# Attention logits in two 64-row tiles of TensorE, two query blocks at a time

## The chip, the cores and the metric

The program runs on one core of one Trainium2 chip. The metric is the device time of one execution in microseconds (us). Engines are named as in the profile: PE is TensorE's matmuls, PEld its weight loads, DVE is VectorE, ACT is ScalarE, POOL is GpSimd, and SP is the queue from which most transfers are issued.

## The reference

A two-layer trunk over a sequence of 2048 frames with width 1024. Layer 0 is a gated pooling mixer. Keys and values are then projected once, keys normalised per head, and layer 1 is a strictly causal stick-breaking attention with 16 heads of 64 elements. Cut to the part that the change touches:

```python
logits = einsum('bhtd,bhsd->bhts', q[:, :, t0:L], k[:, :, :L]) * SB_SCALE      # d = 64
mask = s_idx < t_idx
log_keep = where(mask, log_sigmoid(-logits), 0.0)
later = cumsum(log_keep, reverse=True) - log_keep
log_a = log_sigmoid(logits) + later
a = where(mask, exp(log_a), 0.0)
out = einsum('bhts,bhsd->bhtd', a, v[:, :, :L])
```

All is in 32-bit floating point. The logits contract over the 64 elements of a head only.

## The kernel before, in words

[...] To keep the precision, every operand is split into a high part and a low part (what the high part leaves over), and a product takes three passes: high x high, high x low, low x high.

The program has two parts. The first runs over four chunks of 512 frames (`s` = 0..3): it makes layer 0 and the projections, and writes the queries `qd`, keys `kd` and values `vd`, each as high and low parts, to device memory. The second is the attention. It runs over chunks of 512 queries (`c` = 3, 2, 1, 0), the 16 heads `h`, and chunks of 512 keys `kc` from `c` down to 0. Each triple is a *slot*; there are 64 + 48 + 32 + 16 = 160, and 64 of them (`kc == c`) are diagonal. A slot has four *units*, one for each block `j` of 128 queries. A loop over `n` counts the 640 units, and in each step it emits

- `turn` for the unit six steps back: transposes of 128x128 (L841) from SBUF into a PSUM tile `psa`, which ACT copies to the high part of `at` (L844) and DVE subtracts to the low part (L845);
- `front` for unit `n`: the logits into a PSUM tile `psl` (L816, L817), their sigmoid on ACT into `kap` (L820), and a running product along the keys on DVE into `pp` (L825 in a diagonal slot, L828 in another). In a diagonal slot block `j` has only `(j + 1) * 128` keys;
- a few pieces of the dense products that run beside the attention, from the generator `beside`: the gates `z` during chunk 3, and the output projection and gate of the chunk before during chunks 2, 1 and 0. One piece is one matmul of 128x512 (L885, L887, L889, tile `psd`); `rate` says how many go into a step;
- `gather` for the unit eight steps back: two matmuls with the values (L853, L854, tile `pso`).

When the last chunk's attention is through, the rest of its dense products follow alone.

The logits of a unit take two passes here, over all 128 rows of TensorE. `load_k` puts the key's high part on rows 0 to 63 and its low part on rows 64 to 127 of one tile `kk`. `load_q` makes `qa` (high above low) and `qb` (low above high). The first pass then sums high x high and low x low, and the second adds low x high and high x low. So two blocks take four passes.

There are two buffers of `psl`, two of `psa`, two of `pso`, and four of `kap`. The tiles of queries, keys and values come from one pool, `io`, of ten buffers of 2 KB a row; a slot's tiles are loaded one slot ahead by `begin`. The framework's scheduler sets the order on each engine from this program order, except where `stay` pins an instruction. Once per chunk `c`, `load_ends` makes four transposes of 8 rows (L802, tile `psae`).

Of the kernel before, what the change touches and what calls it, by code (L numbers as in the profile page):

```python
# [8 lines left out]
F32 = mybir.dt.float32  # L9
F32R = mybir.dt.float32r  # L10
# [4 lines left out]
P = 128  # L15
# [4 lines left out]
HD = 64  # L20
PLE = 256
W5 = 512
# [7 lines left out]
def f(ap):  # L30
    return ap.bitcast(F32)
# [3 lines left out]
def trunk_kernel(ctx, tc, x, p, a_norm, a_w_in, a_w_group, a_scale, a_w_out, kv_norm, w_kv,  # L35
                 k_norm, b_norm, b_w_in, b_q_norm, b_w_out, ple_w, ple_gate_w, out):
    nc = tc.nc
    V, A, G, T = nc.vector, nc.scalar, nc.gpsimd, nc.tensor
# [27 lines left out]
    qd = [[dram.tile([P, 2, W5], F32, name=f"qd{s}_{m}") for m in range(NH // 2)] for s in range(NSUB)]  # L66
# [72 lines left out]
    io = ctx.enter_context(tc.tile_pool(name="io", bufs=10))  # L139
# [5 lines left out]
        return act.tile([P, 2, W5], F32R, tag="act", name=nm)  # L145

    def load_q(c, h):
        qa = io.tile([P, W5], F32R, tag="io", name="qa")
        qb = io.tile([P, W5], F32R, tag="io", name="qb")
        rows = qd[c][h // 2][h % 2 * HD : (h % 2 + 1) * HD]  # L150
        for l in range(2):
            nc.sync.dma_start(out=f(qa)[l * HD : (l + 1) * HD], in_=rows[:, l])
            nc.sync.dma_start(out=f(qb)[(1 - l) * HD : (2 - l) * HD], in_=rows[:, l])
        return qa, qb

    def load_k(kc, h):
        kk = io.tile([P, W5], F32R, tag="io", name="kk")
        rows = kd[kc][h // 2][h % 2 * HD : (h % 2 + 1) * HD]
        for l in range(2):
            nc.sync.dma_start(out=f(kk)[l * HD : (l + 1) * HD], in_=rows[:, l])  # L160
        return kk

    def load_v(kc, h):
        vv = io.tile([P, 4, P], F32R, tag="io", name="vv")
# [14 lines left out]
    with ExitStack() as st:  # L179
# [548 lines left out]
        for i, (_, run) in enumerate(steps):  # L728
            after = steps[i + 1][0]() if i + 1 < len(steps) else None
            if after is None:  # L730
                early["q"] = load_q(NSUB - 1, 0)
                early["k"] = [load_k(NSUB - 1, 0), load_k(NSUB - 2, 0)]
                early["w"] = stored(wzd[0])
            run(*ready)
            if not i:
                load_gains([a_scale[0], b_norm[0], kv_norm], gains)
                load_head_gains()
            ready = after
            step, s = i % STEPS, i // STEPS
            if step >= 8 and (s + 1 < NSUB or step < 16):  # L740
                kept.pop(0)()
                if s + 1 < NSUB and step in (8, 12):
                    kept.pop(0)()
# [4 lines left out]
    with ExitStack() as st:  # L748
# [5 lines left out]
        psl = st.enter_context(tc.tile_pool(name="psl", bufs=2, space=bass.MemoryType.PSUM))  # L754
# [38 lines left out]
        def load_ends(c):  # L793
# [12 lines left out]

            return turned

        def front(st, j):

            w = (j + 1) * P if st["diag"] else W5
            r0 = W5 - w
            ps = psl.tile([P, W5], F32, tag="psl", name="psl")
            qs = slice(j * P, (j + 1) * P)
            (qa, qb), kk = st["q"], st["k"]
            T.matmul(ps[:, :w], qa[:, qs], kk[:, :w], start=True, stop=False)  # L816
            T.matmul(ps[:, :w], qb[:, qs], kk[:, :w], start=False, stop=True)  # L817
            kp = kaps[kcount[0] % NK]
            kcount[0] += 1
            A.activation(out=kp[:, r0:], in_=ps[:, :w], func=AF.Sigmoid, scale=-1.0)  # L820

            def scan():
                pp = ppool.tile([P, W5], F32, tag="pp", name="pp")
                if st["diag"]:
                    V.tensor_tensor_scan(out=pp[:, r0:][:, ::-1], data0=kp[:, r0:][:, ::-1],  # L825
                                         data1=ahead[:, r0:][:, ::-1], initial=1.0, op0=ALU.mult, op1=ALU.max)
                else:
                    V.tensor_tensor_scan(out=pp[:, ::-1], data0=kp[:, ::-1], data1=zeros.to_broadcast([P, W5]),  # L828
                                         initial=st["carry"][j], op0=ALU.mult, op1=ALU.add)
                st["carry"][j] = pp[:, r0 : r0 + 1]  # L830
                st["a"].append((pp, r0))

            return scan
# [190 lines left out]
        def begin(i):  # L1024
            c, h, kc = slots[i]
            if kc == c:
                if h == 1:
                    early["ends"] = load_ends(c)
                os = head["os"] if h % 2 else t2.tile([P, W5], F32, tag="os", name="os", bufs=9)
                head.clear()  # L1030
                head.update(q=early.pop("q", None) or load_q(c, h), carry=[None] * 4, o=[], os=os)
            kk = early["k"].pop(0) if early["k"] else load_k(kc, h)
            active[i] = dict(head, c=c, h=h, k=kk, v=load_v(kc, h), diag=kc == c, last=kc == 0, a=[], at={})

        for n in range(4 * len(slots) + LAG_G):
# [4 lines left out]
            i, j = divmod(n, 4)  # L1040
            scan = None
            if i < len(slots):
                c, h, kc = slots[i]
                if j == 0:
                    if i == 0:
                        begin(0)
                    if i + 1 < len(slots):
                        begin(i + 1)
                scan = front(active[i], j)
                if "ends" in early and j == 2:  # L1050
                    early.pop("ends")()
# [58 lines left out]
```

## Time and profile before

| what | value |
|---|---|
| time, median of 3 runs | 2767.84 us (2766.37 to 2770.78) |
| span of the profiled execution | 2765.4 us; that execution's own time is not given apart, and the median lies 2.4 us above its span |
| PE busy | 2725.7 us, 99% of the span, 13715 matmuls |
| PEld busy | 2260.4 us, 82% |
| DVE busy | 1956.0 us, 71% |
| ACT busy | 1385.5 us, 50% |
| POOL busy | 873.7 us, 32% |
| moved by DMA | 573.21 MB, 207 GB/s on average |
| granted TensorE clock | 0.999 |
| attention by chunk of queries, first to last `kap` | c = 3: 1365 to 1866 us; c = 2: to 2215; c = 1: to 2470; c = 0: to 2639 |

A row of the profile names the line, the engine, the operation, the tiles written and read, the shape, the count, the busy time in us and the mean duration of one in ns, and then the idle time before it with what ended it. Matmuls overlap: one of 128x512 lasts about 0.39 us in the records while the next starts 0.23 us after it, so the cost of a matmul is read from the distance between starts, not from its duration. A timeline row gives the start in us from the span's start, then the length, then the instruction; "x4" means four merged into one row.

### The profile page before, as it was taken

What the parts mean: (1) busy time and instruction counts of PE and PEld (TensorE: products, weight loads), DVE (VectorE), ACT (ScalarE), POOL (GpSimd) and SP (SyncE); (2) the same over time, 40 slices, a digit from 0 to 9 for tenths busy, and PEclk for the clock granted to TensorE, in tenths of its full rate; (3) what the DMA queues carried; (4) which work ended last, traced back from release to release, by engine and by line L of the source; (5) the groups of instructions that cost most, each with busy time, mean ns of one, the idle gap of its engine ahead of it and who ended that gap; (6) DMA issues with size and microseconds to landing.
All of it is one profiled execution on the core that took longest, in us unless ns stands there. A gap on an engine that the chain in (4) does not pass through costs nothing. (4 is left out here: it accounts for less than half of the span.)

```text
span 2765.4 us, 39537 instructions
## 1 busy us (share of the span) xinstructions
PE 2725.7 (99%) x13715; PEld 2260.4 (82%) x13715; DVE 1956.0 (71%) x2573; ACT 1385.5 (50%) x2801; POOL 873.7 (32%) x695
## 2 busy tenths in 40 slices
PE   9999999999999999999999999999999999999999
PEld 7888888888888888888888888887887778888877
DVE  6766535655357544565499999999999988996632
ACT  5444532445234542345356566666666655664521
POOL 2574338642475325753121111111110011112220
PEclk9999999999999999999999999999999999999999
DMA  8664696747946479445678565555555566668765
GB/s 293 236 196 171 218 325 204 225 148 253 347 148 227 163 249 318 136 145 170 191 254 278 180 217 170 169 161 178 169 159 162 159 200 200 188 204 264 249 209 160
DMA packets 335835, 573.21 MB, mean 207 GB/s; under 512 B 32462, under 2 KB 166638, under 8 KB 335636
## 3 DMA queue, kind: packets, MB, share of 16 engines
q1 hardware_dynamic: 330186, 563.03, 63.5%
q10 hardware_dynamic: 5450, 7.66, 0.9%
q8 instruction: 108, 1.77, 0.3%
q14 instruction: 91, 0.75, 0.1%
HBM read 430.01 MB, written 132.19 MB: 203 GB/s over the span
## 5 line engine op out<-in xcount | busy, mean ns | idle before, releaser
L844 ACT CAST at<-psa 128x512 fp32r<-128x512 f32 (+3 forms) x640 | 334.1, 522 | 478.4 <-PE psa L841 459.6
L536 PE MATMUL psd<-wpair,x 128*128 128x512 f32 x2304 | 544.0, 393 | 0.0
L828 DVE TENSOR_TENSOR_SCAN pp<-kap,pp,zeros 128x512 f32<-128x512 f32 x384 | 512.9, 1336 | 3.1 <-ACT kap L820 2.4
L536 PEld LDWEIGHTS psd<-wpair,x 128*128 128x128 f32 x2304 | 428.2, 188 | 86.2
L845 DVE TENSOR_TENSOR at<-psa,at 128x512 fp32r<-128x512 f32 (+3 forms) x640 | 381.0, 596 | 88.0 <-ACT at L844 84.9
L841 PE MATMUL psa<-ident,pp 128*128 128x128 f32 x2176 | 347.0, 275 | 17.2 <-DVE at L845 15.5
L820 ACT ACTIVATE kap<-psl 128x512 f32<-128x512 f32 (+3 forms) x640 | 344.9, 539 | 15.1 <-PE psl L817 12.0
L841 PEld LDWEIGHTS psa<-ident,pp 128*128 128x128 f32 x2176 | 262.9, 140 | 93.0 <-DVE at L845 38.8
L816 PE MATMUL psl<-kk,qa 128*128 128x512 f32 (+3 forms) x640 | 281.4, 440 | 0.0
L854 PE MATMUL pso<-at,vv 128*128 128x512 f32 (+3 forms) x640 | 235.1, 367 | 0.0
L817 PE MATMUL psl<-kk,qb 128*128 128x512 f32 (+3 forms) x640 | 233.0, 364 | 0.0
L853 PE MATMUL pso<-at,vv 128*128 128x512 f32 (+3 forms) x640 | 232.7, 364 | 0.0
L825 DVE TENSOR_TENSOR_SCAN pp<-kap,ahead 128x128 f32<-128x128 f32 (+3 forms) x256 | 219.8, 859 | 5.8 <-ACT kap L820 4.1
L131 PE MATMUL psd<-xp,wpair 128*128 128x512 f32 x512 | 201.9, 395 | 1.3 <-ACT xp L269 0.8
L132 PE MATMUL psd<-xp,wpair 128*128 128x512 f32 x512 | 200.5, 392 | 0.0
L133 PE MATMUL psd<-xp,wpair 128*128 128x512 f32 x512 | 200.1, 391 | 0.0
L113 DVE SCALAR_TENSOR_TENSOR wpair<-wraw,gains,wpair 128x512 fp32r<-128x512 f32 x192 | 169.7, 905 | 36.8 <-ACT wpair L112 36.1
L923 POOL TENSOR_TENSOR zr<-zr,sgz 128x512 f32<-128x512 f32 x32 | 58.8, 1836 | 368.2 <-ACT sgz L922 311.3
L112 ACT ACTIVATE wpair<-wraw,gains 128x512 fp32r<-128x512 f32 x192 | 135.0, 720 | 59.0 <-PE psd L536 32.3
L108 POOL TENSOR_TENSOR wpair<-wraw,wpair 128x512 fp32r<-128x512 f32 x99 | 145.5, 1485 | 59.7 <-ACT wpair L106 59.7
L853 PEld LDWEIGHTS pso<-at,vv 128*128 128x128 f32 x640 | 120.2, 188 | 26.9 <-ACT at L844 0.2
L854 PEld LDWEIGHTS pso<-at,vv 128*128 128x128 f32 x640 | 120.3, 188 | 25.9
(211 smaller groups left out, 5402.4 us busy)
## 6 DMA issues: line engine op xcount, KB each, us to landing
kk<-kd SPq DMA_DIRECT2D x320, 128.0 KB
vv<-vd SPq DMA_DIRECT2D x160, 256.0 KB
wraw<-in_w_kv_dram SPq DMA_DIRECT2D x128, 256.0 KB
wpair<-wzd SPq DMA_DIRECT2D x64, 512.0 KB
wpair<-wod SPq DMA_DIRECT2D x64, 512.0 KB
wpair<-wgd SPq DMA_DIRECT2D x64, 512.0 KB
wpair<-wu SPq DMA_DIRECT2D x48, 512.0 KB
wpair<-wi SPq DMA_DIRECT2D x36, 512.0 KB
```

The lines of the kernel that those rows point to most:

```text
L131: T.matmul(ps, wst(units, kt, 0, c0), acts[kt][:, 0], start=(begin and kt == order[0]), stop=False)
L536: T.matmul(pss2[i], ck["x2"][kt][:, xh, tk], wst(ws, kt, wh, 0, W5), start=(kt == 0 and xh == 0 and wh == 0), stop=(kt == KT - 1 and wh == 1))
L816: T.matmul(ps[:, :w], qa[:, qs], kk[:, :w], start=True, stop=False)
L817: T.matmul(ps[:, :w], qb[:, qs], kk[:, :w], start=False, stop=True)
L820: A.activation(out=kp[:, r0:], in_=ps[:, :w], func=AF.Sigmoid, scale=-1.0)
L825: V.tensor_tensor_scan(out=pp[:, r0:][:, ::-1], data0=kp[:, r0:][:, ::-1], data1=ahead[:, r0:][:, ::-1], initial=1.0, op0=ALU.mult, op1=AL ...
L828: V.tensor_tensor_scan(out=pp[:, ::-1], data0=kp[:, ::-1], data1=zeros.to_broadcast([P, W5]), initial=st["carry"][j], op0=ALU.mult, op1=AL ...
L841: T.transpose(pt[:, j * P : (j + 1) * P], pp[:, r0 + kt * P : r0 + (kt + 1) * P], ident)
L844: A.copy(out=at[:, 0, cs], in_=pt[:, cs])
L845: V.tensor_tensor(out=at[:, 1, cs], in0=pt[:, cs], in1=f(at[:, 0, cs]), op=ALU.subtract)
L853: T.matmul(po[:, cs], vv[:, kt, :], at[:, 0, cs], start=(st["diag"] and kt == 0), stop=False)
L854: T.matmul(po[:, cs], vv[:, kt, :], at[:, 1, cs], start=False, stop=(st["last"] and kt == 3))
```

## The change

Two blocks of queries, `j` and `j + 1` for even `j`, get their logits together, by two tiles of 64 rows of TensorE. The tile `e` = 0 stands on rows 0 to 63 and has block `j`; the tile `e` = 1 stands on rows 64 to 127 and has block `j + 1`. Each contracts over 64 rows, so it has three passes (high x high, low x high, high x low; low x low is left out), and the two tiles' passes alternate: six matmuls of 64 rows for two blocks, where four of 128 rows stood.

- `load_q` loads one tile `qt` with even blocks on the upper rows and odd blocks on the lower, high and low parts beside each other: four transfers of 64 KB for a head, in pieces of 512 bytes, where four of 128 KB stood.
- `load_k` loads two tiles, the high and the low part, each twice (on rows 0 to 63 and on rows 64 to 127): four transfers of 128 KB for a slot, where two stood. A slot takes two buffers of `io` for the keys where it took one, and a head one for the queries where it took two.
- `logits` takes both buffers of `psl` at once and writes them for two units; `front` calls it for even `j` only and uses one of the two tiles each time.

```diff
     def load_q(c, h):
-        qa = io.tile([P, W5], F32R, tag="io", name="qa")
-        qb = io.tile([P, W5], F32R, tag="io", name="qb")
-        rows = qd[c][h // 2][h % 2 * HD : (h % 2 + 1) * HD]
+        qt = io.tile([P, 2, 2, P], F32R, tag="io", name="qt")
+        rows = qd[c][h // 2][h % 2 * HD : (h % 2 + 1) * HD].rearrange("d l (g e q) -> e d l g q", e=2, q=P)
+        for e in range(2):
+            for l in range(2):
+                nc.sync.dma_start(out=f(qt)[e * HD : (e + 1) * HD, l], in_=rows[e, :, l])
+        return qt
...
+    def load_k(kc, h):
+        rows = kd[kc][h // 2][h % 2 * HD : (h % 2 + 1) * HD]
+        both = []
         for l in range(2):
-            nc.sync.dma_start(out=f(qa)[l * HD : (l + 1) * HD], in_=rows[:, l])
-            nc.sync.dma_start(out=f(qb)[(1 - l) * HD : (2 - l) * HD], in_=rows[:, l])
-        return qa, qb
...
-            nc.sync.dma_start(out=f(kk)[l * HD : (l + 1) * HD], in_=rows[:, l])
-        return kk
+            kk = io.tile([P, W5], F32R, tag="io", name="kk")
+            for e in range(2):
+                nc.sync.dma_start(out=f(kk)[e * HD : (e + 1) * HD], in_=rows[:, l])
+            both.append(kk)
+        return both
...
+        def logits(st, j):
+            pss = [psl.tile([P, W5], F32, tag="psl", name="psl") for _ in range(2)]
+            qt, (kh, kl) = st["q"], st["k"]
+            for i, (l, kk) in enumerate(((0, kh), (1, kh), (0, kl))):
+                for e in range(2):
+                    w = (j + e + 1) * P if st["diag"] else W5
+                    es = slice(e * HD, (e + 1) * HD)
+                    T.matmul(pss[e][:, :w], qt[es, l, j // 2], kk[es, :w], start=(i == 0), stop=(i == 2))
+            st["l"] = pss
+
         def front(st, j):
...
-            ps = psl.tile([P, W5], F32, tag="psl", name="psl")
-            qs = slice(j * P, (j + 1) * P)
-            (qa, qb), kk = st["q"], st["k"]
-            T.matmul(ps[:, :w], qa[:, qs], kk[:, :w], start=True, stop=False)
-            T.matmul(ps[:, :w], qb[:, qs], kk[:, :w], start=False, stop=True)
+            if j % 2 == 0:
+                logits(st, j)
+            ps = st["l"][j % 2]
```

The order of PE in the middle of chunk 3, before. `psa` are the transposes of an earlier unit, `psl` the logits, `psd` the pieces of the dense product, `pso` the products with the values:

```order
L841 MATMUL psa<-ident,pp 128x128 x4
L816 MATMUL psl<-kk,qa 128x512
L817 MATMUL psl<-kk,qb 128x512
L887 MATMUL psd<-xz,wpair 128x512
L889 MATMUL psd<-xz,wpair 128x512
L885 MATMUL psd<-xz,wpair 128x512
L853 MATMUL pso<-at,vv 128x512
L854 MATMUL pso<-at,vv 128x512
L841 MATMUL psa<-ident,pp 128x128 x4
L816 MATMUL psl<-kk,qa 128x512
L817 MATMUL psl<-kk,qb 128x512
```

The same place after (L855 was L841, L822 is the new line of the logits, L899, L901 and L903 were L885, L887 and L889, L867 and L868 were L853 and L854):

```order
L855 MATMUL psa<-ident,pp 128x128 x4
L822 MATMUL psl<-kk,qt 128x512 x6
L901 MATMUL psd<-xz,wpair 128x512
L903 MATMUL psd<-xz,wpair 128x512
L899 MATMUL psd<-xz,wpair 128x512
L867 MATMUL pso<-at,vv 128x512
L868 MATMUL pso<-at,vv 128x512
L855 MATMUL psa<-ident,pp 128x128 x4
L901 MATMUL psd<-xz,wpair 128x512
L903 MATMUL psd<-xz,wpair 128x512
L899 MATMUL psd<-xz,wpair 128x512
L867 MATMUL pso<-at,vv 128x512
```

The logits of two units stand together in every second unit, between a unit's transposes and a piece of the dense product; in the units between, the pieces follow the transposes directly.

ACT at such a place, before (`at` is the copy of transposes, `kap` the sigmoid of a unit's logits):

```order
L844 CAST at<-psa 128x512
L820 ACTIVATE kap_12820<-psl 128x512
L844 CAST at<-psa 128x512
L820 ACTIVATE kap_12821<-psl 128x512
L844 CAST at<-psa 128x512
L820 ACTIVATE kap_12822<-psl 128x512
```

And after (L858 was L844, L834 was L820):

```order
L858 CAST at<-psa 128x512 x2
L834 ACTIVATE kap_12825<-psl 128x512
L834 ACTIVATE kap_12826<-psl 128x512
L858 CAST at<-psa 128x512 x2
L834 ACTIVATE kap_12827<-psl 128x512
L834 ACTIVATE kap_12828<-psl 128x512
```

Copies and sigmoids alternate two by two where they alternated one by one; DVE's subtractions and running products do the same.

More of the change, by code (lines that the diff above doesn't have):

```diff
@@ L147, in load_q @@
     def load_q(c, h):
-        qa = io.tile([P, W5], F32R, tag="io", name="qa")
-        qb = io.tile([P, W5], F32R, tag="io", name="qb")
-        rows = qd[c][h // 2][h % 2 * HD : (h % 2 + 1) * HD]
-        for l in range(2):
-            nc.sync.dma_start(out=f(qa)[l * HD : (l + 1) * HD], in_=rows[:, l])
-            nc.sync.dma_start(out=f(qb)[(1 - l) * HD : (2 - l) * HD], in_=rows[:, l])
-        return qa, qb
[L156 to L159, printed above, removed]
-            nc.sync.dma_start(out=f(kk)[l * HD : (l + 1) * HD], in_=rows[:, l])
-        return kk
+        qt = io.tile([P, 2, 2, P], F32R, tag="io", name="qt")
[7 more added lines that the diff above has]
+        both = []
+        for l in range(2):
+            kk = io.tile([P, W5], F32R, tag="io", name="kk")
[3 more added lines that the diff above has]
+        return both
     def load_v(kc, h):
```

## The prediction

> **What bounds the kernel now.** I read the page's busy times first, then the costliest groups, then the busy time of each engine in the four stages of the attention, then PE's timeline where the logits stand.
>
> ```profile
> span 2765.4 us, 39537 instructions
> PE 2725.7 (99%) x13715; PEld 2260.4 (82%) x13715; DVE 1956.0 (71%) x2573; ACT 1385.5 (50%) x2801; POOL 873.7 (32%) x695
> L828 DVE TENSOR_TENSOR_SCAN pp<-kap,pp,zeros 128x512 f32<-128x512 f32 x384 | 512.9, 1336 | 3.1 <-ACT kap L820 2.4
> L816 PE MATMUL psl<-kk,qa 128*128 128x512 f32 (+3 forms) x640 | 281.4, 440 | 0.0
> L825 DVE TENSOR_TENSOR_SCAN pp<-kap,ahead 128x128 f32<-128x128 f32 (+3 forms) x256 | 219.8, 859 | 5.8 <-ACT kap L820 4.1
> ```
>
> PE is busy 99% of the span. The counts give the work: 640 units, of which 384 are full (L828) and 256 belong to 64 diagonal slots (L825). The stages of the attention, one for each chunk of queries from c = 3 to c = 0:
>
> ```profile
> core 0: us, PE busy (x) PEld busy (x) DVE busy (x) ACT busy (x) POOL busy (x), PEclk, DMA share, GB/s
> 1365.00:1866.00 501.00, 497.42 (x2707) 414.06 (x2706) 472.94 (x563) 300.11 (x598) 76.46 (x44) 1.00 0.65 204
> 1866.00:2215.00 349.00, 338.79 (x1880) 276.88 (x1879) 343.59 (x432) 226.33 (x466) 39.29 (x24) 1.00 0.55 166
> 2215.00:2470.00 255.00, 249.06 (x1388) 208.96 (x1386) 230.86 (x304) 154.34 (x335) 35.30 (x24) 1.00 0.65 196
> 2470.00:2639.00 169.00, 167.05 (x907) 141.32 (x905) 114.79 (x178) 85.11 (x205) 32.49 (x23) 1.00 0.79 245
> ```
>
> PE sets the pace in stages 3, 1 and 0. In stage 2 it is DVE (343.6 of 349 us), and PE idles 10.2 us there. So a change of PE's work counts in full in three stages; in stage 2 a gain is worth at most DVE's 5.4 us of idle time, and the first 10 us of a loss are hidden.
>
> **What the logits cost before.** A full unit of stage 3 on PE:
>
> ```profile
> 1701.24 0.60 PE L841 MATMUL psa<-ident,pp 128*128 128x128 f32 x4
> 1701.59 0.48 PE L816 MATMUL psl<-kk,qa 128*128 128x512 f32 x1
> 1701.91 0.39 PE L817 MATMUL psl<-kk,qb 128*128 128x512 f32 x1
> 1702.13 0.40 PE L887 MATMUL psd<-xz,wpair 128*128 128x512 f32 x1
> 1702.37 0.40 PE L889 MATMUL psd<-xz,wpair 128*128 128x512 f32 x1
> 1702.61 0.39 PE L885 MATMUL psd<-xz,wpair 128*128 128x512 f32 x1
> 1702.83 0.40 PE L853 MATMUL pso<-at,vv 128*128 128x512 f32 x1
> 1703.07 0.40 PE L854 MATMUL pso<-at,vv 128*128 128x512 f32 x1
> ```
>
> From L817 to L854 five starts take 1.16 us, so a pass of 128x512 costs 0.232 us whatever its duration. Two blocks of a full slot take four passes: 0.93 us. From the transposes to the second dense piece (L889) it is 1.13 us here; less the two passes of logits (0.464), 0.666 us is left for the transposes and one piece. Taken off the same stretch in a diagonal slot, that gives the narrower passes:
>
> ```profile
> 1707.44 0.60 PE L841 MATMUL psa<-ident,pp 128*128 128x128 f32 x4
> 1707.79 0.30 PE L816 MATMUL psl<-kk,qa 128*128 128x128 f32 x1
> ...
> 1708.33 0.39 PE L889 MATMUL psd<-xz,wpair 128*128 128x512 f32 x1
> ...
> 1709.26 0.60 PE L841 MATMUL psa<-ident,pp 128*128 128x128 f32 x4
> 1709.61 0.36 PE L816 MATMUL psl<-kk,qa 128*128 128x256 f32 x1
> ...
> 1710.17 0.39 PE L889 MATMUL psd<-xz,wpair 128*128 128x512 f32 x1
> ...
> 1711.09 0.60 PE L841 MATMUL psa<-ident,pp 128*128 128x128 f32 x4
> 1711.44 0.42 PE L816 MATMUL psl<-kk,qa 128*128 128x384 f32 x1
> ...
> 1712.11 0.39 PE L889 MATMUL psd<-xz,wpair 128*128 128x512 f32 x1
> ```
>
> 128 keys: 0.89 - 0.666 = 0.22 us for two passes; 256 keys: 0.24; 384 keys: 0.35. The first is hardly cheaper than the second: below 256 keys the weight load sets the pace, some 0.11 us each. The first two blocks of a diagonal slot take 0.47 us, the last two 0.35 + 0.46 = 0.82.
>
> **What a change of the tile's rows costs.** The kernel has one kind of matmul today that does not use all 128 rows: the four transposes of 8 rows (L802), and one of 24 rows early on (L657).
>
> ```profile
> 2226.69 0.40 PE L817 MATMUL psl<-kk,qb 128*128 128x512 f32 x1
> 2227.02 0.32 PEld L802 LDWEIGHTS psae<-ident,ends 8*128 8x128 f32 x4 [0.36 <-issue]
> ...
> 2227.36 0.19 PEld L885 LDWEIGHTS psd<-x,wpair 128*128 128x128 f32 x1
> 2227.36 0.50 PE L885 MATMUL psd<-x,wpair 128*128 128x512 f32 x1
> ...
> 2227.70 0.39 PE L887 MATMUL psd<-x,wpair 128*128 128x512 f32 x1
> ...
> 2473.70 0.34 PE L817 MATMUL psl<-kk,qb 128*128 128x384 f32 x1
> ...
> 2473.97 0.32 PEld L802 LDWEIGHTS psae<-ident,ends 8*128 8x128 f32 x4 [0.25 <-issue]
> ...
> 30.81 0.60 PE L206 MATMUL pst<-ident,rx 128*128 128x128 f32 x4
> ...
> 31.34 0.13 PEld L657 LDWEIGHTS pst<-ident,grow 24*128 24x128 f32 x1 [0.17 <-issue]
> ```
>
> Among matmuls of 128 rows the next weights load while the last matmul streams. Here they don't. After L817 (512 columns, 0.232 us) the 8-row weights start 0.33 us after its start, so 0.10 after its stream is over; after the one of 384 columns (0.175 us) they start at 0.27, again 0.10 after. After transposes of 128 rows the 24-row weights start 0.20 us after the start of the fourth (30.81 + 3 x 0.11 = 31.14), of which 0.11 is its own cost: 0.09. No engine or transfer is named as the releaser (the rows say "issue"). On the way out, L885's weights and its matmul both start at 2227.36, and the next starts 0.34 us later where 0.232 is usual: its weight load, hidden otherwise, shows with 0.105 us. So a change costs about 0.10 us of waiting, and the first weights after it stand exposed. The four 8-row loads take 0.32 us, 0.13 for the last, so they follow each other at 0.06 us.
>
> No row shows a tile of 64 rows. That a change between 128 and 64 rows waits as one between 128 and 32 or fewer does is taken from these rows as the nearest. [...]
>
> **The change part by part.** Every group of six matmuls stands between transposes and a dense piece, both of 128 rows, so it has two changes: 320 groups, 640 changes. For a weight load of 64 rows I take 0.06 (the 8-row loads) to 0.11 us (128 rows). The streams of the two tiles: 3 x 0.232 if they run side by side, 6 x 0.232 if one after the other. I take the first, since a pass costs by its columns and the tiles share neither rows nor output bank; the other end is a rival.
>
> - Full pairs, 192 groups: 0.10 (in) + one to two loads (0.06 to 0.22; the second tile may start one load later) + 0.70 + 0.10 (out) + 0.105 (exposed weights) = 1.06 to 1.22 us, against 0.93. That is +0.13 to +0.29, middle 0.21: +25 to +56 us, **+40**.
> - First two blocks of a diagonal slot, 64 groups: three passes of 256 columns (0.37) with one load, or six loads in a row (0.66) with a last pass of 0.12, beside 0.305 for the changes: 0.73 to 1.08, against 0.47. +0.26 to +0.61: +17 to +39 us, **+28**.
> - Last two blocks, 64 groups: 1.06 to 1.22 against 0.82: +0.24 to +0.40: +15 to +26 us, **+20**.
> - Cover in stage 2: **-10 us**, PE's idle time there.
> - Buffers of `psl`: a group needs both, so it waits for the sigmoid of the unit just before. In ACT's order the two sigmoids follow the group directly: some 0.2 + 2 x 0.60 us (0.61 in the stage's rows), while PE has at least two units of transposes, pieces and gathers, 2 x 1.6 us, until the next group. The cover is 1.8 us; if ACT's other work ate it, each group would pay up to its 0.6 us. I take nothing, and up to +10 us.
> - Keys are loaded in four transfers of 128 KB for a slot instead of two, queries in half the bytes. That is 160 x 256 KB - 64 x 256 KB = 25 MB more over 1274 us, 20 GB/s on 166 to 245. PE waits for no transfer there today and slots are loaded one ahead (about 8 us in stages 3 to 1). SP issues 320 more transfers, and behind them stand weights of the dense pieces. Nothing, with up to +5 us.
>
> Together 40 + 28 + 20 - 10 = **+78 us**, with bounds of +47 and +126. The profiled span of 2765.4 becomes 2843.4; the median lies 2.4 us over that span, so the time is **2846 us**.
>
> **The rivals.**
>
> *The change of rows costs nothing with 64-row tiles, and it is faster.* Then a full pair has three passes for four: -0.232 x 192 = -45 us; a diagonal slot -0.22 to +0.07, in the middle -5 us in all; of that, 10 us fall into stage 2, where DVE allows only 5 of 15. About -40 us: 2728. It decides at the point where the two changes of a group cost under 50 / 320 = 0.16 us together; the rows above give 0.31 and the first weights besides. For it speaks only that no row has 64 rows. Chance 0.10.
>
> *The two tiles don't run side by side*, and the changes cost as above. Six passes one after the other add 0.70 x 192 = 134 us in full pairs and some 0.8 x 64 = 51 in diagonal slots to the +78: about 3030 us. The trace has no two tiles in flight and is silent. [...] Chance 0.10.
>
> *One after the other, but no wait at the change*: (6 - 4) x 0.232 x 192 = 89 us, diagonal slots 0.63 x 64 = 40, less 10: +119, 2887. Chance 0.05. *Only the weights stand exposed and nothing drains*: 0.20 x 320 = 64 us less than forecast, about +16: 2784. Chance 0.05.
>
> **How the numbers follow.** The forecast has a chance of 0.70, with its own bounds from 2815 to 2894. Leaving out the first two rivals (0.10 each), the range takes in the other two: 2784 to 2894. A measurement of this kernel tells about 0.2% (5 us) from no change. Faster has the first rival and a little of small changes, 0.11; the same 0.02; slower 0.87.
>
> **What would show it.** Right: weights of the first 64-row matmul start about 0.2 us after the last transpose's start, and those of the dense piece after a group 0.33 us after the last logits matmul; the two tiles' matmuls start within 0.11 us of each other and the passes of one tile 0.23 us apart; stage 3 takes about 533 us, stage 2 365, stage 1 274, stage 0 181; DVE's idle time grows. Wrong: weights for 64 rows that load under the transposes before them; a group of six that takes 1.4 us of streams; PE waiting for ACT at the logits; or a stage 2 that grows as much as its PE work.

## The result and the profile after

The changed kernel takes 2836.1 us (median of 4 runs, 2835.71 to 2837.03) against 2768.0 us before in the same comparison: 1.0245 times as long, 95% interval 1.0230 to 1.0259, or +68 us. The forecast was 2846 us, +78.

The page's head and the group of the logits, and the four stages of the attention at their new bounds:

```profile
span 2834.4 us, 41303 instructions
PE 2796.6 (99%) x14355; PEld 2209.6 (78%) x14355; DVE 1965.2 (69%) x2573; ACT 1401.6 (49%) x2801; POOL 874.8 (31%) x695
L822 PE MATMUL psl<-kk,qt 64*128 64x512 f32 (+3 forms) x1920 | 295.7, 396 | 0.3
```
```profile
core 0: us, PE busy (x) PEld busy (x) DVE busy (x) ACT busy (x) POOL busy (x), PEclk, DMA share, GB/s
1366.00:1890.00 524.00, 521.82 (x2960) 389.85 (x2960) 477.59 (x564) 304.51 (x598) 76.27 (x44) 1.00 0.74 219
1890.00:2260.00 370.00, 360.78 (x2072) 262.42 (x2070) 344.64 (x430) 228.88 (x465) 38.11 (x23) 1.00 0.59 178
2260.00:2531.00 271.00, 265.40 (x1524) 200.13 (x1524) 236.68 (x308) 159.59 (x337) 36.38 (x24) 1.00 0.67 200
2531.00:2705.00 174.00, 171.74 (x946) 135.38 (x945) 112.40 (x174) 86.75 (x203) 32.56 (x23) 1.00 0.77 238
```

PE is still busy 99%, and PEld, with 640 loads more, is busy less. All four stages grew: 501 to 524, 349 to 370, 255 to 271, 169 to 174 us; outside the attention some 3 us were added. DVE's work is nearly the same and its idle time grew, from 28 to 46 us in stage 3 and from 5 to 25 in stage 2.

PE and PEld around one group, first of a full slot, then (PE only) of the first and of the last two blocks of a diagonal slot:

```profile
1705.68 0.60 PE L855 MATMUL psa<-ident,pp 128*128 128x128 f32 x4
...
1706.21 0.53 PEld L822 LDWEIGHTS psl<-kk,qt 64*128 64x128 f32 x6 [0.17 <-issue]
1706.21 0.96 PE L822 MATMUL psl<-kk,qt 64*128 64x512 f32 x6
...
1707.10 0.19 PEld L903 LDWEIGHTS psd<-xz,wpair 128*128 128x128 f32 x1 [0.36 <-issue]
1707.10 0.50 PE L903 MATMUL psd<-xz,wpair 128*128 128x512 f32 x1
...
1707.44 0.39 PE L899 MATMUL psd<-xz,wpair 128*128 128x512 f32 x1
```
```profile
1432.41 0.60 PE L855 MATMUL psa<-ident,pp 128*128 128x128 f32 x4
...
1432.94 0.62 PE L822 MATMUL psl<-kk,qt 64*128 64x128 f32 x6
...
1433.83 0.39 PE L901 MATMUL psd<-x,wpair 128*128 128x512 f32 x1
```
```profile
1436.12 0.60 PE L855 MATMUL psa<-ident,pp 128*128 128x128 f32 x4
1436.64 0.96 PE L822 MATMUL psl<-kk,qt 64*128 64x384 f32 x6
...
1437.88 0.40 PE L899 MATMUL psd<-x,wpair 128*128 128x512 f32 x1
```

The fourth transpose starts at 1706.01 (1705.68 + 3 x 0.11) and costs 0.11, so the weights at 1706.21 start 0.09 us after it: PE waits, with no releaser named. The first weights of both tiles load together, in the time of one:

```profile
1706.21 0.18 PEld L822 LDWEIGHTS psl<-kk,qt 64*128 64x128 f32 x2 [0.17 <-issue]
```

Six matmuls last 0.96 us together, where six in a row would have started over 1.16 us and then lasted 0.39 more: the tiles run side by side. The exit shows as forecast: the dense piece's weights and matmul start together at 1707.10, and the next one 0.34 us later. From the transposes to the second piece is 1.76, 1.42 and 1.76 us; less the 0.666 for transposes and a piece, a group costs **1.09, 0.75 and 1.09 us**, where the passes before cost 0.93, 0.47 and 0.82. Times 192, 64 and 64 groups that is 31 + 18 + 17 = 66 us more work for PE. The medians over all groups come to 1.09, 0.75 and 1.10 us, which makes 67.

### The profile page after: what moved, and what is told of

Same layout as the page of the kernel before. It is cut to its first block, busy times and chain, and to the rows that moved or that the text cites. A ratio compares the mean times of both kernels' runs of the same rounds, so it can differ in the third digit from the quotient of the medians.

```text
span 2834.4 us, 41303 instructions
## 1 busy us (share of the span) xinstructions
PE 2796.6 (99%) x14355; PEld 2209.6 (78%) x14355; DVE 1965.2 (69%) x2573; ACT 1401.6 (49%) x2801; POOL 874.8 (31%) x695
## 5 line engine op out<-in xcount | busy, mean ns | idle before, releaser
L858 ACT CAST at<-psa 128x512 fp32r<-128x512 f32 (+3 forms) x640 | 333.9, 522 | 456.6 <-PE psa L855 445.9
L842 DVE TENSOR_TENSOR_SCAN pp<-kap,pp,zeros 128x512 f32<-128x512 f32 x384 | 501.4, 1334 | 21.1 <-ACT kap L834 20.3
L859 DVE TENSOR_TENSOR at<-psa,at 128x512 fp32r<-128x512 f32 (+3 forms) x640 | 373.2, 596 | 108.9 <-ACT at L858 106.0
L834 ACT ACTIVATE kap<-psl 128x512 f32<-128x512 f32 (+3 forms) x640 | 320.3, 533 | 83.8 <-PE psl L822 71.7
L855 PE MATMUL psa<-ident,pp 128*128 128x128 f32 x2176 | 345.8, 274 | 13.3 <-DVE at L859 12.6
L855 PEld LDWEIGHTS psa<-ident,pp 128*128 128x128 f32 x2176 | 265.3, 141 | 81.7 <-DVE at L859 26.2
L822 PE MATMUL psl<-kk,qt 64*128 64x512 f32 (+3 forms) x1920 | 295.7, 396 | 0.3
L868 PE MATMUL pso<-at,vv 128*128 128x512 f32 (+3 forms) x640 | 234.4, 366 | 0.0
L867 PE MATMUL pso<-at,vv 128*128 128x512 f32 (+3 forms) x640 | 233.4, 365 | 0.0
L822 PEld LDWEIGHTS psl<-kk,qt 64*128 64x128 f32 x1920 | 158.9, 185 | 67.5 <-issue 52.0
L867 PEld LDWEIGHTS pso<-at,vv 128*128 128x128 f32 x640 | 120.4, 188 | 28.2 <-issue 1.5
L868 PEld LDWEIGHTS pso<-at,vv 128*128 128x128 f32 x640 | 120.5, 188 | 27.0
```

Of the source, the lines that this page charges most:

```text
L822: T.matmul(pss[e][:, :w], qt[es, l, j // 2], kk[es, :w], start=(i == 0), stop=(i == 2))
L855: T.transpose(pt[:, j * P : (j + 1) * P], pp[:, r0 + kt * P : r0 + (kt + 1) * P], ident)
L858: A.copy(out=at[:, 0, cs], in_=pt[:, cs])
L859: V.tensor_tensor(out=at[:, 1, cs], in0=pt[:, cs], in1=f(at[:, 0, cs]), op=ALU.subtract)
L867: T.matmul(po[:, cs], vv[:, kt, :], at[:, 0, cs], start=(st["diag"] and kt == 0), stop=False)
L868: T.matmul(po[:, cs], vv[:, kt, :], at[:, 1, cs], start=False, stop=(st["last"] and kt == 3))
```

## The experiments

The theory: the change of the tile's rows costs about 0.2 us each way, 640 times, and that is more than the passes saved. Against it stand that the tiles don't overlap, that issuing two units at once is what costs, and that the loads do. Differences are against the kernel before in the same comparison (medians 2768.0 to 2769.5 us).

**e1: two units at once, without 64-row tiles.** In the kernel before:

```diff
-            ps = psl.tile(...)                     # two passes for unit j
+            if j % 2 == 0:                         # four passes for units j and j + 1
+                st["l"] = [psl.tile(...) for _ in range(2)]
+                ...
+            ps = st["l"][j % 2]
```

> The kernel before with one thing of the change alone: the logits of two units are issued together, four passes over all 128 rows, into both buffers of psl; loads and tiles as before. Theory (the change of rows is what costs): PE's work is the same, so about 2768 us, at most 2778 if stage 2 suffers from sigmoids and running products going two by two. Rival (taking both buffers at once makes PE or DVE wait): a good part of the 68 us that the change cost, over 2790.

2782.3 us, +12.8 (ratio 1.0044, 1.0029 to 1.0059). Neither guess: not the bulk, but not nothing. Stage 2 grew from 349 to 360 us, stages 3 and 1 by 1 and 2 us, and stage 0 became 2 us shorter. What PE waited for in stage 2 (total in us, times, longest), before and in e1:

```profile
PE psa L841 <- DVE at L845: 8.9, 19, 1.6
```
```profile
PE psa L845 <- DVE at L849: 18.8, 27, 2.0
```

**e3: three entries and exits for each group.** In the changed kernel:

```diff
                     T.matmul(pss[e][:, :w], qt[es, l, j // 2], kk[es, :w], start=(i == 0), stop=(i == 2))
+                if i < 2:
+                    next(filler, None)
+                    owed -= 1.0
```

> The changed kernel with a piece of the dense product, taken from those that follow anyway, between the three pairs of 64-row matmuls of a group: three entries into 64-row tiles and three exits for each group instead of one. Theory: two more of each, 2 x (0.093 wait + 0.107 weights in, 0.09 + 0.107 out) = 0.79 us for each of 320 groups: +254 us on 2836, about 3090. Rival (the cost sits in the group as a whole or in its buffers): within 20 us of 2836.

3075.3 us, 239 over the changed kernel for 640 further entries and exits: 0.37 us for one of each. On PE's timeline of e3 a pair of 64-row matmuls and a dense piece alternate at 0.43 us each, where 0.232 is the cost of a stream:

```profile
1703.37 0.50 PE L823 MATMUL psl<-kk,qt 64*128 64x512 f32 x2
1703.80 0.50 PE L907 MATMUL psd<-xz,wpair 128*128 128x512 f32 x1
1704.23 0.50 PE L823 MATMUL psl<-kk,qt 64*128 64x512 f32 x2
1704.67 0.50 PE L903 MATMUL psd<-xz,wpair 128*128 128x512 f32 x1
```

So a change costs 0.19 us by the time and 0.20 us by these rows, in and out alike, for a group of two matmuls as for one of six. The rival that the cost sits in the group is out.

**e4: both tiles on the same rows.**

```diff
-                    es = slice(e * HD, (e + 1) * HD)
+                    es = slice(0, HD)
```

> The changed kernel with both blocks' matmuls on rows 0 to 63 (odd blocks then get the logits of even ones, so this computes something else); same number of matmuls, same entries and exits. Theory (the two tiles run side by side in the changed kernel): all six passes follow each other, +0.70 x 192 + 0.35 x 64 + 0.52 x 64 = +190 us: about 3026. Rival (the tiles do not overlap, their starts are only recorded together): no change, 2836.

2999.3 us, 163 over the changed kernel. PE's groups by form, changed kernel and then e4:

```profile
L822 PE MATMUL psl<-kk,qt 64*128 64x512 f32 x1344 | 251.8, 427 | 0.0
```
```profile
L822 PE MATMUL psl<-kk,qt 64*128 64x512 f32 x1344 | 394.3, 406 | 0.0
```

The same 1344 matmuls of 512 columns cover 252 us in one case and 394 in the other. A full group costs 1.78 us instead of 1.09: the 0.69 that the theory asks for. Summed over all groups that is 187 us, 24 more than the 163. Of these, some 15 us are waits of PE for DVE that are gone in e4 (19.8 us in the attention of the changed kernel, 4.4 in e4; 8 of the 15 in stage 2); the other 9 are not settled. That the two tiles run side by side is shown.

**e10: passes ordered by tile**, three of the upper rows and then three of the lower:

```diff
-            for i, (l, kk) in enumerate(((0, kh), (1, kh), (0, kl))):
-                for e in range(2):
+            for e in range(2):
+                for i, (l, kk) in enumerate(((0, kh), (1, kh), (0, kl))):
```

> The changed kernel with the passes ordered by tile: three of the upper rows, then three of the lower, instead of alternating; same matmuls, same entries and exits. Theory (matmuls start in program order, so two tiles overlap only where neighbours in the order are on different rows): one pass in three overlaps, five steps instead of three: +0.46 x 192 + 0.23 x 64 + 0.35 x 64 = +126 us: about 2962. Rival (each tile goes on by itself whatever the order): 2836.

2857.4 us (two runs): +21 on the changed kernel, not +126. The theory fell here and its rival was nearly right. The matmuls of one group in e10 that start in its first tenth of a microsecond, by form (PE):

```profile
L822 PE MATMUL psl<-kk,qt 64*128 64x512 f32 x1 | 0.5, 493 | 0.0
L822 PE MATMUL psl<-kk,qt 64*128 64x384 f32 x1 | 0.4, 437 | 0.0
```

In the built program, too, the three of 384 columns come first and those of 512 are the fourth to sixth, yet the first of each starts at once. A group costs 1.10 us as before, so the two tiles each go through their own matmuls; by these rows the fourth of the program starts with the first, where the theory had all starts in the program's order. The 21 us are explained in part: the groups make 2; PE's waits for DVE's subtractions come to 22.0 us in the attention, where the changed kernel has 12.6; and 4 us lie ahead of the attention, whose first `kap` starts at 1370.2 instead of 1366.1. Why the waits are longer is open.

**e2 and e7: three passes of 128 rows and no change of rows.** In the changed kernel (e7 also holds PE's, ACT's and DVE's order to the program's):

```diff
+            w = (j + 2) * P if st["diag"] else W5
...
-                for e in range(2):
-                    ...
-                    T.matmul(pss[e][:, :w], qt[es, l, j // 2], kk[es, :w], start=(i == 0), stop=(i == 2))
+                T.matmul(pss[i % 2][:, :w], qt[:, l, j // 2], kk[:, :w], start=(i < 2), stop=(i > 0))
```

> The changed kernel with its order and loads, but each group is three passes over all 128 rows instead of six of 64 (the logits are then mixed from two blocks, so this computes something else). It is the count of passes that the change aims at, without a change of rows. Theory: the passes saved count, 0.232 x 192 + 0.22 x 64 = 59 us less than before: 2709 us; if DVE bounds stage 2 as the prediction said, 13 us of that are lost there: 2722. Rival (grouping or the loads cost): not below 2755.

> The three passes of 128 rows for two blocks of e2 (another computation), with PE's, ACT's and DVE's orders held to the program's, so that the dense pieces are spread as in the kernel before; in e2 the scheduler bunched up to 48 of them. Theory (passes saved count where PE sets the pace): stage 3 -26 us, stage 1 -11, stage 0 -4, stage 2 at most -5 since DVE is busy there: about 2725 us. Rival (the pair form holds the attention back whatever PE does): 2780 or more, as e2 had it.

e2 took 2824.7 us (ratio 1.0192, 1.0175 to 1.0209), which its rival's bound (not below 2755) allows; e6 below, with the same loads and four passes for two blocks, took 2789.0. The scheduler put up to 24 dense pieces in a row in stage 3 and 48 in stage 0. In stage 2 it did not, and yet PE waits most there. Its waits for DVE's subtractions in stages 3 and 2 of e2:

```profile
PE psa L853 <- DVE at L857: 32.8, 38, 2.4
PE psa L853 <- DVE at L857: 36.9, 39, 2.4
```

Besides, the granted clock of e2 is 0.50 in nine stretches of 3.4 us of the attention, where the kernel before has none. So the bunched pieces are at most a part of it, and the rest is open. With all orders held, e7 took 2769.6 us, the time of the kernel before (1.0004, 0.9994 to 1.0013). Both of its guesses missed: 59 us of PE's passes are gone and the time is the same. The kernel to set it against is e11 below, which has the same loads and the same holds and four passes. The four stages of e11, then of e7:

```profile
1366.00:1878.00 512.00, 500.41 (x2708) 415.42 (x2709) 470.82 (x563) 296.28 (x598) 72.27 (x43) 0.99 0.77 225
1878.00:2235.00 357.00, 340.91 (x1879) 278.82 (x1877) 345.18 (x432) 223.13 (x464) 37.64 (x24) 1.00 0.62 185
2235.00:2493.00 258.00, 251.04 (x1388) 210.98 (x1387) 229.77 (x304) 152.21 (x336) 34.24 (x23) 0.99 0.70 209
2493.00:2667.00 174.00, 169.33 (x903) 143.24 (x903) 112.05 (x177) 83.95 (x205) 31.19 (x23) 0.98 0.80 239
```
```profile
1366.00:1868.00 502.00, 479.97 (x2580) 394.39 (x2581) 469.29 (x563) 304.96 (x599) 75.19 (x44) 0.99 0.78 229
1868.00:2223.00 355.00, 330.50 (x1785) 263.86 (x1784) 344.96 (x432) 229.91 (x466) 36.12 (x24) 0.99 0.62 187
2223.00:2472.00 249.00, 240.88 (x1325) 200.91 (x1324) 229.97 (x304) 157.31 (x335) 35.16 (x23) 0.99 0.71 215
2472.00:2644.00 172.00, 165.31 (x871) 137.99 (x870) 113.31 (x178) 86.05 (x205) 31.03 (x23) 0.99 0.76 242
```

The passes taken out bring 25 us: 10 in stage 3 (of 26 by count), 2 in stage 2 (of 18), 9 in stage 1 (of 11), 2 in stage 0. PE now idles 22 us in stage 3 and 24 in stage 2, where DVE is busy 345 of 355. PE's waits in the attention are 39 us in e11 and 60 in e7: 10 of the 21 more are for DVE's subtractions and 7 for weights. That leaves some 13 of the 34 us which the 59 did not bring unsettled. The longest wait of e7 is not DVE's:

```profile
1416.45 0.27 PE L803 MATMUL psa<-ident,pp 128*128 128x128 f32 x1
1425.13 1.65 PE L800 MATMUL psd<-x,wpair 128*128 128x512 f32 x3 [8.41 <-DMA wpair<-wzd]
```

**e8: one needless pass more for each two units**, in the kernel before:

```diff
+            if j % 2 == 0:
+                T.matmul(ps[:, :w], qb[:, qs], kk[:, :w], start=True, stop=True)
             T.matmul(ps[:, :w], qa[:, qs], kk[:, :w], start=True, stop=False)
```

> The kernel before with one needless pass of 128 rows more for each two units (it is overwritten), so no change of rows and no new order. It prices PE's time: 0.232 x 192 + (0.11 + 0.175) x 64 = 63 us of passes, 19 of them in stage 2. Theory (PE sets the pace but for about 10 us of cover in stage 2): +53 us, 2822. Rival (no cover at all): +63, 2832. Other rival (PE is not the bound, and the changed kernel lost its time otherwise): under +30.

2817.3 us, +48.6 (1.0181, 1.0164 to 1.0198) for 63 us of passes, 5 under the first theory. Stage 2 grew by 12 of 19, stage 3 by 23 of 27. So PE sets the pace for added work, and some 14 us are hidden, half of them in stage 2.

**e5 and e9: copies and sigmoids one by one again**, in e1 and in the changed kernel, by pinning the sigmoid, the copy, the subtraction and the running product to the program's order:

```diff
-            A.activation(out=kp[:, r0:], in_=ps[:, :w], func=AF.Sigmoid, scale=-1.0)
+            stay(A.activation(out=kp[:, r0:], in_=ps[:, :w], func=AF.Sigmoid, scale=-1.0))
```

> The pairs of e1 (four passes of 128 rows for two blocks, issued together), with ACT's and DVE's order held to the program's, so that copies and sigmoids, subtractions and running products alternate one by one as in the kernel before. Theory (the 13 us of e1 come from two running products in a row, which delay the subtractions that free psa, so that PE waits in stage 2): back to 2769 +- 3 us, and stage 2 from 360 to 350 us. Rival (the 13 us come from both buffers of psl taken at once): the logits now wait for the sigmoid behind a copy, and it stays at 2782 or gets slower.

> The changed kernel with ACT's and DVE's order held to the program's, one by one instead of two by two; everything else as changed. Theory (the order two by two costs its part here too): what e5 gained on e1, some 8 us, mostly in stage 2: 2828. Rival (PE has so much work here that the order no longer matters): 2836 +- 2.

e5 took 2774.0 us, +5.3 (1.0018, 1.0008 to 1.0027): more than half of e1's 12.8 come from the order two by two. Stage 2 fell from 360 to 355, not to 350, and PE's wait there from 18.8 us in e1 to 13.5:

```profile
PE psa L845 <- DVE at L849: 13.5, 25, 1.4
```

e9 took 2831.2 us (1.0229, 1.0214 to 1.0244): 5 us under the changed kernel, with intervals that overlap; stage 2 went from 370 to 366. It is the fastest form of the change here, and slower than the kernel before.

**e6, e11 and e12: the changed kernel's loads by themselves**, with four passes of 128 rows:

```diff
+            for e in range(2):
+                w = (j + e + 1) * P if st["diag"] else W5
+                for l, kk in ((0, kh), (1, kl)):
+                    T.matmul(pss[e][:, :w], qt[:, l, j // 2], kk[:, :w], start=(l == 0), stop=(l == 1))
```

> The changed kernel's loads and order, but four passes of 128 rows for two blocks as in e1 (products of other halves, so this computes something else). It differs from e1 in the loads alone: keys loaded twice, queries in half the bytes and in pieces of 512 bytes. Theory (transfers are hidden): as e1, 2782 +- 3 us. Rival (the loads cost): 5 us or more above e1.

> As e6 (the changed kernel's loads, four passes of 128 rows for two blocks, another computation) with PE's, ACT's and DVE's orders held to the program's; to be set against e12, which differs in the loads alone and has the same order on PE. Theory (doubled key loads delay something, as e6 against e1 hinted): about 6 us above e12. Rival (e6 differed by its bunched dense pieces): within 2 us of e12.

> As e5 (loads of the kernel before, four passes of 128 rows for two blocks, sigmoids and running products one by one) with PE's order held to the program's too. Both theories: as e5, 2774 +- 3 us.

e6 took 2789.0 us (1.0076, 1.0061 to 1.0091), 7 over e1, as the rival that the loads cost had it. e12 took 2785.1 (1.0060, 1.0045 to 1.0075), 11 over e5, so holding PE's order has a price of its own, which I had not expected. The rows show most of it: PE's wait at the transposes `psao` of the tile `sg`, which DVE writes, in e5 and in e12, and the two longest stretches of e12 in which the granted clock (the third number from the end) is 0.50.

```profile
PE psao L990 <- DVE sg L984: 2.8, 2, 1.4
```
```profile
PE psao L798 <- DVE sg L993: 7.7, 2, 4.5
```
```profile
2250.50:2257.30 6.80, 4.26 (x17) 3.69 (x17) 1.83 (x4) 1.67 (x3) 1.26 (x1) 0.50 0.68 203
2509.90:2516.70 6.80, 5.40 (x19) 4.74 (x20) 3.27 (x6) 3.30 (x7) 0.53 (x1) 0.50 0.86 275
```

PE, held to the program's order, waits 5 us more for DVE (7.7 against 2.8), and the granted clock is 0.50 in these two stretches of 6.8 us, around the two waits, and in one more of 3.4 us; e5 has no such stretch in the attention (mean granted clock 0.999 in e5, 0.996 in e12). An estimate from these rows is 5 us of waiting and some 6 of slower matmuls. e11 and e7 have the same two waits, 7.7 and 8.0 us, so this hardly touches their comparison. e11 took 2794.7 (1.0097, 1.0080 to 1.0114), 10 over e12. In e11 and e12 all heads of stage 3 but the second and fourth take the same time within 0.01 us a unit; the second takes 8 us longer in e11, and PE waits 6.1 us there for `wpair`, one of the weight tiles that SP issues behind the doubled key loads. It happens once, at the start of the attention. In the changed kernel PE's matmuls wait for no transfer in the attention and its logits' weights for 0.5 us, so there the loads cost nothing that shows; the changed kernel without the doubled loads was not run.

## Why the prediction was right

The sign and the mechanism held: the wait at each change of rows is 0.09 us and the first weights stand exposed for 0.11, as the few 8-row and 24-row matmuls of the kernel before had it, and e3 priced a change at 0.19 us by the time alone. That 64-row tiles pay what smaller ones pay was the step with the least behind it, taken from rows of 8 and 24; it is now shown: the wait of 0.09 us stands where 128 rows give way to 64 (weights at 1706.21). That the two tiles run side by side, with no wait where they alternate, was an estimate of mine that no row of the kernel before shows; in the changed kernel the six matmuls last 0.96 us together, the first weights of the two tiles load in 0.18 us together, and e4, with both blocks on the same rows, takes 163 us more.

By the terms of the sum:

- Full pairs +40: measured +31. Last two blocks of a diagonal slot +20: +17. First two +28: +18. All three lie near the low ends. The mis-sized term is mainly the second tile's weight load, for which I took the middle of "one to two loads"; both tiles' weights load at the same time (two loads in 0.18 us). The two waits are 0.18 us together, by what is left of 1.09 after 0.70 of streams and two exposed loads of 0.105, where the forecast had 0.20.
- Cover in stage 2, -10: e8 hides about 14 us of added work in all, 7 of it in stage 2. Right in kind, though in the changed kernel itself the cover doesn't show (below).
- Buffers of `psl`, 0 with up to +10: wrong, +12.8 by e1, of which 10.7 in stage 2. The prediction asked only what PE's logits wait for; the cost came by DVE, whose two running products in a row delay the subtractions that free `psa`. e5 shows for more than half of it that the order two by two is the cause; the remainder is not settled.
- Loads, 0: by PE's waits this held in the changed kernel; in the forms with four passes the loads cost 7 to 10 us (e6, e11).

67 - 14 + 13 = 66 us against 68 measured. That the overestimate of the groups and the omitted order two by two partly cancelled is luck: stage 2 was forecast at 365 us and took 370, stages 3, 1 and 0 at 533, 274 and 181 and took 524, 271 and 174.

One of the prediction's signs of being wrong did come true: stage 2 grew by 21 us, for 19 us of added work of PE (64 x 0.16 + 32 x 0.28). The forecast of 10 us of cover there failed in the changed kernel. That the loss by the order two by two (10.7 us in e1) and the cover cancel is argued from e1 and e8. PE's wait for DVE's subtractions in stage 2 is 8.1 us in the changed kernel, where it was 8.9 before:

```profile
PE psa L855 <- DVE at L859: 8.1, 13, 1.7
```

Two slips of the prediction change nothing: 78 less 64 is 14, so its fourth rival's time is 2782 us and not 2784; and L657 has two more matmuls of few rows, of 8 and of 2.

The first rival, that without a cost of the change the kernel would be 40 us faster, was too good too. By e7 against e11 the passes are worth 25 us, since DVE and a few waits take over a part of the pace as soon as PE has less to do, and the price of issuing two units at once goes off that: e1's 13 us, or e5's 5 with sigmoids and running products one by one. An estimate from these runs: had the changes cost nothing, some 12 us faster in the form of the change and some 20 in the form of e9; at 640 changes, each would have had to cost under 0.02 or 0.03 us.

## What to carry to other kernels

Before splitting TensorE into row tiles, count how often the stream goes in and out of them: here each crossing cost 0.19 to 0.20 us, nearly as much as a whole pass of 512 columns (0.232), so a group here would have had to save nearly two passes to pay. A rare instruction elsewhere in the trace (four transposes of 8 rows) can price a mechanism before it is built. And a count of passes saved is worth its time only as far as the next engine, and the waits on it, allow: adding 63 us of passes cost 49, and taking 59 away brought 25.

## What the runs showed of the hardware that I had not expected

- The two row tiles each kept their own order: with the matmuls of one tile all ahead of the other's in the program, both tiles still started within 0.1 us and a group cost 1.10 us against 1.09 (e10).
- The weights of the two row tiles loaded at the same time: two loads in 0.18 us, where the median of a single one is 184 ns (changed kernel).
- Around two waits of PE in e12, of 4.5 and 3.2 us, the granted clock was 0.50 for 6.8 us each, and PE was busy for 4.26 and 5.40 us of these.
